# Two-layer network on one core: expert weights fetched one expert per slot in 4 KB rows, scatters in one batch

## The chip, the cores and the metric

The program runs on one core of one Trainium2 chip. The metric is the device time of one execution in microseconds (us). The core has a matrix engine (TensorE: PE for its matmuls, PEld for the loads of their stationary operand), a vector engine (DVE), an activation engine (ACT), GpSimd (POOL) and a queue engine (SP) that here only issues transfers. Sixteen DMA engines move data between the off-chip memory and the on-chip buffer of 128 partitions.

## What is computed

A token block of 256 rows and 1024 features goes through two layers, and then through a second block (forget-gate attention, a convolutional feed-forward and a gated addition). Each of the two layers has a mixer, a layer norm, a mixture of 16 experts, and a layer norm again. The experts are what the change touches:

```python
probs_g = softmax(xf @ w_group + b_group)              # 4 groups, the best one is taken
p_top, g_idx = top_k(probs_g, 1)
in_group = logits_e[group g_idx]                       # 4 experts of that group
w_top, e_local = top_k(softmax(in_group), 2)           # two of them
gates = p_top * w_top / sum(w_top)                     # zero for the other 14 experts
h = silu(x @ w_gate[e]) * (x @ w_up[e])                # 1024 -> 256, for each expert e
y = sum over e of (h * gates[e]) @ w_down[e]           # 256 -> 1024
```

All numbers are 32-bit floats. A layer has 16 x 3 x 1 MB of expert weights, and every expert's weights are read.

## The kernel before

`forward` (line 1230) runs a layer as mixer, output projection, `moe_slots` (line 728) and layer norm. In `moe_slots` the 256 tokens are two halves `tt` of 128. Each expert has room for `CAP` = 32 tokens of each half. A matrix `Pm[tt]` of zeros and ones (token by expert place) is made from the routing; `gather` (line 750) multiplies the normed tokens, split into a high part `xh` and a low part `xl`, by it: for a block `k` of 128 features, the stationary operand is `xh[:, tt, ks]`, a block of 128 neighbouring features, and the result, features by 512 expert places, is written to `XG[tt][k]` with the layer norm's scale and offset, which are columns of the constant `cw` (`mix_col`).

The 16 experts are taken in four groups `q` of four. `gate_up(q, ks, tt)` multiplies, for each block `k` and each expert `i` of the group, the 32 gathered tokens by 128 rows of gate and up weights. The four experts' results lie in the four 32-partition strips of one bank of the accumulator, so four matmuls run beside one another. `hidden` applies the gate's silu and the token's weight, `turned` transposes, `expert_down(q, hf, tt)` multiplies by half `hf` (512 columns) of the down weights and splits the result into a high part `yh` and a low part `yl`, and `scatter` adds them to the token's rows with two matmuls (lines 926 and 927).

Weights come in slots of 1 MB (8 KB in each partition). One layer uses 48 of them, in this order for each group: eight for gate and up, four for down. They are taken from three sets of buffers, in the order that the string `ORDER` (line 25) writes out: 7 of a ring, 4 more of `moe_slots`, and 2 that a pair of activation tiles leaves free; 2 more come free when the gathers are done with `xh` and `xl`. A slot is filled again only when its reader is done, and SP issues the transfers one after the other, each waiting for its own slot. So 13 to 15 slots are ahead of PE.

- `gate_up4` (line 676) fills a slot with one feature block `k` of four experts: two transfers of 512 KB, in which each row that is moved at one time is 256 numbers, 1 KB.
- A down slot (line 960) holds 128 rows of 512 columns of four experts: rows of 2 KB.
- A gate and up slot comes free after `gate_up` of its `k` for the second half; the slots of a group come free one by one.

PE's order is written out by hand (`seq` keeps it). After the first gathers: `gate_up(0, 0..3, 0)`, the other gathers, `gate_up(0, 0..3, 1)`, the weights of the scatter (lines 884 and 885), and then for each group: the rest of `gate_up`, **two blocks of the next group's `gate_up` for the first half** (line 964), the two transposes, the two `late` scatters of the group before, three `expert_down`, two scatters, the fourth `expert_down`. The last group ends with its own four scatters in two lots. At `q == 1`, `then` loads the next layer norm's two parameter rows, 512 KB each, over POOL's queue.

The scale row `gnb` of the first mixer (`hgrn`) is loaded in `consts`, at the start, on ACT's queue.

Of the kernel before, what the change touches and what calls it, by code (L numbers as in the profile page):

```python
# [8 lines left out]
F32 = mybir.dt.float32  # L9
# [37 lines left out]
class Net:  # L47
# [35 lines left out]
    def consts(self):  # L83
# [10 lines left out]
        self.gnb = t([P, 768], F32, "gnb")  # L94
        nc.scalar.dma_start(self.gnb, I["a_gnorm"][0].partition_broadcast(P))
# [352 lines left out]
    def hgrn(self, xT, wk):  # L448
        nc, I, V = self.nc, self.I, self.nc.vector
        W = I["a_w_in"][0]  # L450
        mm = nc.tensor.matmul
        Ss, Sm = [], []
# [11 lines left out]
        for j in range(3):  # L464
# [75 lines left out]
            nc.gpsimd.tensor_tensor(gs, gs, self.gnb[:, None, j * 256:j * 256 + 256].to_broadcast([P, 2, 256]),  # L540
# [187 lines left out]
    def moe_slots(self, xs, stats, lnw, layer, proj, then):  # L728
# [3 lines left out]
        with self.work() as wk:  # L732
# [16 lines left out]

            def gather(tt, k, dve):  # L750

                if k % 2 == 0:
                    XGT[tt].append(self.spl_tile(("hi", "lo")[tt], F32))
                ks = slice(k * P, (k + 1) * P)
# [5 lines left out]
                gc, bc = (self.mix_col(layer, n, k) for n in range(2))  # L760
# [5 lines left out]
            def lead():  # L766
# [49 lines left out]
                A, B = slice(0, 256), slice(256, 1024)  # L816
# [45 lines left out]
            def gate_up(q, ks, tt):  # L862

                for k in ks:
                    if (q, k) not in gu:
                        gu[q, k] = self.gate_up4(slot(), layer, q, k)
# [9 lines left out]
            for k in range(4):  # L876
                gu[0, k] = self.gate_up4(slot(), layer, 0, k)
# [34 lines left out]
            def expert_down(q, hf, tt):  # L912

                yb = self.bank()
                for f in range(2):
                    for i in range(4):
                        seq(mm(yb[CAP * i:CAP * i + CAP, :], hT[tt][:, f, CAP * i:CAP * i + CAP],  # L917
                               wd[q][2 * hf + f][:, i], start=f == 0, stop=f == 1))
                yh = wk.tile([P, 512], F32R, tag="yh", name=self.nm("yh"), bufs=2)
                yl = wk.tile([P, 512], F32R, tag="yl", name=self.nm("yl"), bufs=2)  # L920
# [453 lines left out]
```

## Time and profile before

| | |
|---|---|
| time, median of 3 runs | 965.22 us (964.32 to 966.99) |
| the profiled execution | 964.35 us, its span 962.8 us |
| PE busy | 880.5 us, 91% of the span |
| PE's weight loads | 652.9 us, 68% |
| DVE, ACT, POOL busy | 54%, 40%, 4% |
| moved by DMA | 207.09 MB, mean 215 GB/s |
| clock granted to PE | 0.962 of full speed on average |

The span is what the profiler saw of one execution; the time reported for that execution is 1.55 us longer. PE's share of busy time is an average over stages with quite different limits. The stages are told apart by the 40 slices of the profile's second part: the mixers, projections and the feed-forward move 54 to 250 GB/s, and in the two expert stages (about 203 to 318 us and 473 to 588 us) the DMA line stands at 350 to 370 GB/s.

### The profile page before, as it was taken

To read this page: it belongs to the slowest core of one execution; us is meant where nothing else is said; L and a number is where in the kernel's file an instruction comes from. 1 tells how busy PE (TensorE), PEld (TensorE's weight loads), DVE (VectorE), ACT (ScalarE), POOL (GpSimd) and SP (SyncE) were. 2 spreads that over 40 slices of the span, in tenths; PEclk is the share of its full clock that TensorE was granted. 3 is DMA by queue.
4 is the path that set the end of the run, shared out by engine and by line. 5 is a ranking of instruction groups with operands and counts; after the bars stand their busy time and mean duration, and the time that the engine had idled before them with its cause. 6 is when DMAs were issued, how large, how long until landed. Compare 5 with 4: busy or idle time off the path is not lost.

```text
span 962.8 us, 16096 instructions
## 1 busy us (share of the span) xinstructions
PE 880.5 (91%) x6733; PEld 652.9 (68%) x6733; DVE 517.3 (54%) x859; ACT 388.8 (40%) x628; POOL 36.8 (4%) x85
## 2 busy tenths in 40 slices
PE   5999989999869799989997697999998999999996
PEld 5899978742223497767532134888777999999975
DVE  5577784662101855655521027564468656656685
ACT  4443744351001355543611013564455545545531
POOL 2010110000000100000000000000000000000000
PEclk9999999999879899999897898999999999999998
DMA  9944335959999963319599999633245755556201
GB/s 320 350 137 149 116 119 178 321 189 368 352 362 372 339 203 109 102 54 302 176 364 352 366 365 351 221 132 100 88 133 181 254 176 176 185 170 214 88 1 69
DMA packets 163391, 207.09 MB, mean 215 GB/s; under 512 B 10231, under 2 KB 132719, under 8 KB 163311
## 3 DMA queue, kind: packets, MB, share of 16 engines
q1 hardware_dynamic: 162416, 203.43, 63.7%
q0 software_dynamic: 576, 2.10, 0.6%
q8 instruction: 55, 0.90, 0.4%
q10 hardware_dynamic: 318, 0.45, 0.2%
q14 instruction: 26, 0.21, 0.1%
HBM read 204.91 MB, written 1.05 MB: 214 GB/s over the span
## 4 chain that ended last, share of the span: by engine, by line
PE 81%; DVE 6%; DMA 6%; ACT 3%; issue 2%; POOL 1%; SPq 0%; ACTq 0%; POOLq 0%; DVEq 0%
PE pb L869 11%; PE pb L199 9%; PE pb L201 9%; PE pb L200 9%; PE pb L205 8%; PE pb L207 8%; PE pb L206 8%; PE pb L917 5%; DMA w<-in_w_up_dram 4%; PE pb L1004 2%; DVE lo L189 1%; DMA fx_wf<-in_attn_w_in_dram 1%; PE pb L271 1%; ACT hi L187 1%; PE pb L756 1%
## 5 line engine op out<-in xcount | busy, mean ns | idle before, releaser
L189 DVE TENSOR_TENSOR lo<-w,hi 128x1024 fp32r<-128x1024 f32 x151 | 184.2, 1223 | 102.0 <-ACT hi L187 101.0
L187 ACT ACTIVATE hi<-w 128x1024 fp32r<-128x1024 f32 x151 | 158.8, 1057 | 131.5 <-PE pb L201 63.2
L199 PE MATMUL pb<-th,hi 128*128 128x256 f32 x728 | 210.1, 289 | 0.7 <-ACT hi L187 0.6
L200 PE MATMUL pb<-th,lo 128*128 128x256 f32 x728 | 209.4, 288 | 0.7 <-DVE lo L189 0.7
L201 PE MATMUL pb<-tl,hi 128*128 128x256 f32 x728 | 208.8, 287 | 0.0
L199 PEld LDWEIGHTS pb<-th,hi 128*128 128x128 f32 x728 | 141.5, 194 | 4.7 <-issue 2.9
L200 PEld LDWEIGHTS pb<-th,lo 128*128 128x128 f32 x728 | 141.5, 194 | 2.5 <-issue 1.1
L201 PEld LDWEIGHTS pb<-tl,hi 128*128 128x128 f32 x728 | 141.6, 194 | 2.0 <-issue 2.0
L205 PE MATMUL pb<-hi,th 128*128 128x256 f32 (+1 forms) x308 | 107.8, 350 | 2.4 <-ACT th L261 1.4
L207 PE MATMUL pb<-hi,tl 128*128 128x256 f32 (+1 forms) x308 | 107.0, 347 | 0.3 <-DVE tl L262 0.3
L206 PE MATMUL pb<-lo,th 128*128 128x256 f32 (+1 forms) x308 | 106.8, 347 | 0.0
L869 PE MATMUL pb<-w,hi 128*32 128x512 f32 x512 | 67.2, 653 | 28.0 <-DMA w<-in_w_up_dram 28.0
L205 PEld LDWEIGHTS pb<-hi,th 128*128 128x128 f32 x308 | 59.8, 194 | 9.3 <-ACT th L261 2.3
L207 PEld LDWEIGHTS pb<-hi,tl 128*128 128x128 f32 x308 | 59.2, 192 | 9.3 <-DVE tl L262 2.0
L261 ACT ACTIVATE yh<-pb 128x512 fp32r<-128x512 f32 x32 | 19.1, 598 | 112.6 <-PE pb L917 100.5
L206 PEld LDWEIGHTS pb<-lo,th 128*128 128x128 f32 x308 | 59.5, 193 | 6.8 <-issue 0.7
L869 PEld LDWEIGHTS pb<-w,hi 128*32 128x32 f32 x512 | 16.0, 115 | 69.8 <-issue 67.3
L869 PE MATMUL pb<-w,lo 128*32 128x512 f32 x512 | 59.0, 592 | 0.0
L917 PE MATMUL pb<-w,hT 128*32 128x512 f32 x512 | 58.3, 596 | 0.6 <-DVE hT L909 0.6
L189 DVE TENSOR_TENSOR wdl<-w,wdh 128x1024 fp32r<-128x1024 f32 x25 | 30.5, 1224 | 39.1 <-ACT wdh L187 39.1
L262 DVE TENSOR_TENSOR yl<-pb,yh 128x512 fp32r<-128x512 f32 x32 | 22.1, 690 | 53.5 <-ACT yh L261 53.5
L187 ACT ACTIVATE wdh<-w 128x1024 fp32r<-128x1024 f32 x25 | 26.4, 1059 | 48.4 <-PE pb L207 44.4
(334 smaller groups left out, 1190.5 us busy)
## 6 DMA issues: line engine op xcount, KB each, us to landing
w<-in_w_gate_dram SPq DMA_DIRECT2D x64, 512.0 KB, 9.0
w<-in_w_up_dram SPq DMA_DIRECT2D x64, 512.0 KB, 8.8
w<-in_w_down_dram SPq DMA_DIRECT2D x32, 1024.0 KB, 11.3
w<-in_ffn_w_up_dram SPq DMA_DIRECT2D x22, 1024.0 KB, 5.1
w<-in_a_w_in_dram SPq DMA_DIRECT2D x13, 1024.0 KB, 10.0
w<-in_attn_w_in_dram SPq DMA_DIRECT2D x12, 1024.0 KB, 8.5
w<-in_ffn_w_down_dram SPq DMA_DIRECT2D x11, 1024.0 KB, 4.9
w<-in_w_o_dram SPq DMA_DIRECT2D x8, 1024.0 KB, 5.0
```

The lines of the kernel that those rows point to most:

```text
L187: a = nc.scalar.activation(h, src, AF.Copy)
L189: b = nc.vector.tensor_sub(l, src, h)
L199: mm(out, ah, bh, start=first, stop=False)
L200: mm(out, al, bh, start=False, stop=False)
L201: mm(out, ah, bl, start=False, stop=last)
L205: mm(out, xh, wh, start=first, stop=False)
L206: mm(out, xh, wl, start=False, stop=False)
L207: mm(out, xl, wh, start=False, stop=last)
L262: i = self.nc.vector.tensor_sub(l, ps, h)
L869: seq(mm(gb[q][tt][CAP * i:CAP * i + CAP, :], XG[tt][k][:, c:c + CAP], gu[q, k][:, i], start=k == 0, stop=k == KT - 1))
L917: seq(mm(yb[CAP * i:CAP * i + CAP, :], hT[tt][:, f, CAP * i:CAP * i + CAP], wd[q][2 * hf + f][:, i], start=f == 0, stop=f == 1))
L1004: nc.tensor.matmul(o(h), v[:, 0, vc(h)], ATs[h][:, 0:256], start=True, stop=False)
```

## The change

- A gate and up slot holds one expert (`gate_up_rows`): half `g` of its 1024 features, for gate and up. Partition `p` gets the four neighbouring rows `512 g + 4 p` to `512 g + 4 p + 3`, which are 4 KB in one piece in memory. Four slots (`fetch(q, g)`) are one half of a group. A transfer is 512 KB as before, in 128 rows of 4 KB.
- So block `k` of the features is no longer 128 neighbours, but every fourth one of 512: `gather` takes its stationary operand with a step of 4 numbers (`rows4`), and the scale and offset columns come from a new constant `mixp`, loaded at the start in the same order by four transfers on ACT's queue, 16 bytes at a time.
- A down slot holds one expert's whole down weight: 256 rows of 4 KB, one transfer of 1 MB.
- PE's order: the two blocks of the next group ahead of `turned` are gone; all four scatters of a group are late, and run as one batch in the next group after its first `turned`. For that `yh` and `yl` have three buffers instead of two, and the fourth pair uses the buffers of `Pm`.
- `gnb` is loaded in `hgrn`'s own buffers.
- The low and high parts in `lead` are made in two pieces of 512 columns instead of 256 and 768.

```diff
@@ consts
-        self.gnb = t([P, 768], F32, "gnb")
-        nc.scalar.dma_start(self.gnb, I["a_gnorm"][0].partition_broadcast(P))
+        self.mixp = t([P, 2, 2, 8], F32, "mixp")
+        for i, n in enumerate(("ln_mix_g", "ln_mix_b")):
+            for layer in range(2):
+                nc.scalar.dma_start(self.mixp[:, layer, i].rearrange("p (g r) -> p g r", g=2),
+                                    I[n][layer].rearrange("(g p r) -> p g r", g=2, r=4))
@@ hgrn
+        gnb = wk.tile([P, 768], F32, tag="gnb", name=self.nm("gnb"))
+        nc.scalar.dma_start(gnb, I["a_gnorm"][0].partition_broadcast(P))
@@
-    def gate_up4(self, slot, layer, q, k):
-        v = slot.rearrange("p (e c) -> p e c", e=4)
+    def gate_up_rows(self, slot, layer, e, g):
+        v = slot.rearrange("p (w r c) -> p w r c", w=2, r=4)
         for i, w in enumerate(("w_gate", "w_up")):
-            self.nc.sync.dma_start(v[:, :, i * 256:(i + 1) * 256],
-                                   self.I[w][layer, 4 * q:4 * q + 4, k * P:(k + 1) * P].rearrange("e p c -> p e c"))
+            self.nc.sync.dma_start(v[:, i], self.I[w][layer, e, 512 * g:512 * g + 512].rearrange("(p r) c -> p r c", r=4))
         return v
@@ moe_slots
+            def rows4(x, tt, k):
+                return x[:, tt, 512 * (k // 4):512 * (k // 4) + 512].rearrange("t (p r) -> t r p", r=4)[:, k % 4]
...
-                seq(mm(gb, xh[:, tt, ks], Pm[tt], start=True, stop=False))
-                seq(mm(gb, xl[:, tt, ks], Pm[tt], start=False, stop=True))
+                seq(mm(gb, rows4(xh, tt, k), Pm[tt], start=True, stop=False))
+                seq(mm(gb, rows4(xl, tt, k), Pm[tt], start=False, stop=True))
...
-                A, B = slice(0, 256), slice(256, 1024)
+                A, B = slice(0, 512), slice(512, 1024)
...
+            def fetch(q, g):
+                gu[q, g] = [self.gate_up_rows(slot(), layer, 4 * q + i, g) for i in range(4)]
+
+            def gate_up(q, g, tt):
+                if (q, g) not in gu:
+                    fetch(q, g)
+                for k in range(4 * g, 4 * g + 4):
                     for i in range(4):
                         c = (4 * q + i) * CAP
-                        seq(mm(gb[q][tt][CAP * i:CAP * i + CAP, :], XG[tt][k][:, c:c + CAP], gu[q, k][:, i],
-                               start=k == 0, stop=k == KT - 1))
+                        seq(mm(gb[q][tt][CAP * i:CAP * i + CAP, :].rearrange("p (w c) -> p w c", w=2),
+                               XG[tt][k][:, c:c + CAP], gu[q, g][i][:, :, k % 4], start=k == 0, stop=k == KT - 1))
...
             for q in range(4):
+                sg = []
                 if q:
-                    gate_up(q, range(2), 1)
-                    gate_up(q, range(2, 4), 0)
-                    gate_up(q, range(2, 4), 1)
-                gate_up(q, hi4, 0)
-                sg = [hidden(q, 0)]
-                gate_up(q, hi4, 1)
-                sg.append(hidden(q, 1))
+                    gb[q] = [self.bank("j"), self.bank("j")]
+                    for tt in range(2):
+                        gate_up(q, 0, tt)
+                for tt in range(2):
+                    gate_up(q, 1, tt)
+                    sg.append(hidden(q, tt))
                 if q == 1:
                     then()
                 wd[q] = []
-                for n in range(4):
-                    wd[q].append(slot().rearrange("p (e c) -> p e c", e=4))
-                    nc.sync.dma_start(wd[q][n], I["w_down"][layer, 4 * q:4 * q + 4, n % 2 * P:(n % 2 + 1) * P,
-                                                            n // 2 * 512:(n // 2 + 1) * 512].rearrange("e p c -> p e c"))
-                if q < 3:
-                    gb[q + 1] = [self.bank("j"), self.bank("j")]
-                    gate_up(q + 1, range(2), 0)
-                hT = [turned(sg[tt]) for tt in range(2)]
+                for i in range(4):
+                    wd[q].append(slot().rearrange("p (f c) -> p f c", f=2))
+                    nc.sync.dma_start(wd[q][i], I["w_down"][layer, 4 * q + i].rearrange("(f p) c -> p f c", p=P))
+                hT = [turned(sg[0])]
                 for y in late:
                     scatter(q - 1, *y)
-                if q < 3:
-                    y = [expert_down(q, 0, 0), expert_down(q, 0, 1), expert_down(q, 1, 0)]
-                    for n in range(2):
-                        scatter(q, *y[n])
-                    late = [y[2], expert_down(q, 1, 1)]
...
+                if q:
+                    hT.append(turned(sg[1]))
+                late = [expert_down(q, hf, 0) for hf in range(2)]
+                if not q:
+                    hT.append(turned(sg[1]))
+                late.append(expert_down(q, 0, 1))
+                if q == 3:
+                    for y in late[:2]:
+                        scatter(q, *y)
+                late.append(expert_down(q, 1, 1))
+            for y in late[2:]:
+                scatter(3, *y)
```

## Rows read from the trace of the kernel before

**Rows 1.** The page's part 4, the chain that ended last: shares by engine, by line.
```profile
PE 81%; DVE 6%; DMA 6%; ACT 3%; issue 2%; POOL 1%; SPq 0%; ACTq 0%; POOLq 0%; DVEq 0%
PE pb L869 11%; PE pb L199 9%; PE pb L201 9%; PE pb L200 9%; PE pb L205 8%; PE pb L207 8%; PE pb L206 8%; PE pb L917 5%; DMA w<-in_w_up_dram 4%; PE pb L1004 2%; DVE lo L189 1%; DMA fx_wf<-in_attn_w_in_dram 1%; PE pb L271 1%; ACT hi L187 1%; PE pb L756 1%
```

**Rows 2.** Line 869 (gate and up matmuls): PE's idle time before them (releaser: us, times).
```profile
  DMA w<-in_w_up_dram: 28.0, 8
```

**Rows 3.** The chain, layer 0's expert stage: start us, us, engine, tile, line, count.
```profile
202.11 3.57 PE pb L869 x32
...
236.93 9.34 DMA w<-in_w_up_dram
...
246.40 1.93 PE pb L869 x8
...
259.41 12.06 PE pb L869 x112
...
271.55 9.65 DMA w<-in_w_up_dram
...
308.77 5.29 PE pb L917 x48
...
317.60 1.06 ACT hi L187
```

**Rows 4.** The chain, layer 1's expert stage.
```profile
471.41 3.57 PE pb L869 x32
...
541.54 9.34 DMA w<-in_w_up_dram
...
587.26 1.06 ACT hi L187
```

**Rows 5.** SP's queue in time: transfers issued (start us, us of issue, line, tile, count).
```profile
201.90 0.37 SPq L960 DMA_DIRECT2D w<-in_w_down_dram  x1
203.17 0.53 SPq L680 DMA_DIRECT2D w<-in_w_gate_dram  x1
...
472.46 0.37 SPq L680 DMA_DIRECT2D w<-in_w_gate_dram  x1
```

**Rows 6.** Windows: us, engines' busy (x), granted clock, DMA share, GB/s. 1 KB, then 2 KB rows.
```profile
293.00:294.00 1.00, 1.00 (x16) 0.39 (x12) 0.00 (x0) 0.00 (x0) 0.00 (x0) 1.00 1.11 350
...
265.00:266.00 1.00, 1.00 (x12) 0.26 (x8) 0.00 (x0) 0.00 (x0) 0.00 (x0) 1.00 1.06 389
...
269.00:270.00 1.00, 1.00 (x16) 0.30 (x12) 0.00 (x0) 0.00 (x0) 0.00 (x0) 1.00 1.04 383
```

**Rows 7.** Windows of lone 1 MB transfers: 4 KB rows (feed-forward down), then 1 KB rows (up).
```profile
842.07:842.57 0.50, 0.50 (x4) 0.38 (x4) 0.50 (x1) 0.05 (x1) 0.00 (x0) 1.00 0.97 401
842.57:843.07 0.50, 0.50 (x4) 0.41 (x3) 0.50 (x2) 0.00 (x0) 0.00 (x0) 1.00 1.05 434
843.07:843.57 0.50, 0.50 (x4) 0.34 (x3) 0.39 (x1) 0.00 (x0) 0.00 (x0) 1.00 1.01 418
...
850.07:850.57 0.50, 0.50 (x6) 0.50 (x6) 0.50 (x2) 0.46 (x2) 0.00 (x0) 1.00 1.09 387
```

**Rows 8.** The DMA view: the layer norm parameters that `then` loads, over POOL's queue.
```profile
lng<-in_ln_ffn_g_dram POOLq DMA_DIRECT2D x2, 512.0 KB, 7.1
```

**Rows 9.** A window within the first stall: PE's granted clock is the third number from the right.
```profile
245.00:246.00 1.00, 0.00 (x0) 0.00 (x0) 0.00 (x0) 0.00 (x0) 0.00 (x0) 0.50 1.10 348
```

**Rows 10.** Gather's loads (ns min/median/max); a chain row of gather; a window where loads fill PEld.
```profile
L756 PEld LDWEIGHTS pb<-Pm,th x32: 186/188/333, 189.1 to 470.5; 128*128 128x128 f32 x32
...
198.15 0.23 PE pb L757
...
340.00:350.00 10.00, 10.00 (x83) 9.88 (x82) 5.34 (x5) 5.28 (x8) 0.00 (x0) 1.00 0.79 263
```

**Rows 11.** A transfer of 1024 rows of 64 bytes: its issue on SP, and a window it fell in.
```profile
576.19 2.50 SPq L1092 DMA_DIRECT2D fx_wf<-in_attn_w_in_dram  x1
...
585.00:586.00 1.00, 1.00 (x12) 0.26 (x8) 1.00 (x3) 0.00 (x0) 0.00 (x0) 1.00 1.11 315
```

**Rows 12.** The timeline at the start: ACT's first work, and the DVE row the chain passes through.
```profile
3.19 1.28 ACT L261 ACT_TABLE_LOAD   x1 [3.19 <-issue]
...
9.43 0.68 DVE L262 TENSOR_TENSOR tl<-pb,th 128x512 fp32r<-128x512 f32 x1
```

More of the change, by code (lines that the diff above doesn't have):

```diff
@@ L539, in hgrn @@
                     V.tensor_mul(gs[:, tt], gb[tt], gs[:, tt])
-            nc.gpsimd.tensor_tensor(gs, gs, self.gnb[:, None, j * 256:j * 256 + 256].to_broadcast([P, 2, 256]),
+            nc.gpsimd.tensor_tensor(gs, gs, gnb[:, None, j * 256:j * 256 + 256].to_broadcast([P, 2, 256]),
                                     op=ALU.mult)
@@ L753, in gather @@
                     XGT[tt].append(self.spl_tile(("hi", "lo")[tt], F32))
-                ks = slice(k * P, (k + 1) * P)
                 gb = self.bank("a")
-                seq(mm(gb, xh[:, tt, ks], Pm[tt], start=True, stop=False))
-                seq(mm(gb, xl[:, tt, ks], Pm[tt], start=False, stop=True))
+                seq(mm(gb, rows4(xh, tt, k), Pm[tt], start=True, stop=False))
+                seq(mm(gb, rows4(xl, tt, k), Pm[tt], start=False, stop=True))
                 o = XGT[tt][k // 2][:, k % 2 * 512:k % 2 * 512 + 512]
                 XG[tt].append(o)
-                gc, bc = (self.mix_col(layer, n, k) for n in range(2))
+                gc, bc = (self.mixp[:, layer, n, k:k + 1] for n in range(2))
                 if dve:
@@ L860, in lead @@
                 yield
[L862 to L866, printed above, removed]
+            def fetch(q, g):
[4 more added lines that the diff above has]
+                for k in range(4 * g, 4 * g + 4):
                     for i in range(4):
                         c = (4 * q + i) * CAP
-                        seq(mm(gb[q][tt][CAP * i:CAP * i + CAP, :], XG[tt][k][:, c:c + CAP], gu[q, k][:, i],
-                               start=k == 0, stop=k == KT - 1))
+                        seq(mm(gb[q][tt][CAP * i:CAP * i + CAP, :].rearrange("p (w c) -> p w c", w=2),
+                               XG[tt][k][:, c:c + CAP], gu[q, g][i][:, :, k % 4], start=k == 0, stop=k == KT - 1))
             hook = lead()
@@ L875, in moe_slots @@
             gb[0] = [self.bank("j"), self.bank("j")]
-            for k in range(4):
-                gu[0, k] = self.gate_up4(slot(), layer, 0, k)
+            fetch(0, 0)
             proj(hook)
@@ L917, in expert_down @@
                         seq(mm(yb[CAP * i:CAP * i + CAP, :], hT[tt][:, f, CAP * i:CAP * i + CAP],
-                               wd[q][2 * hf + f][:, i], start=f == 0, stop=f == 1))
-                yh = wk.tile([P, 512], F32R, tag="yh", name=self.nm("yh"), bufs=2)
-                yl = wk.tile([P, 512], F32R, tag="yl", name=self.nm("yl"), bufs=2)
+                               wd[q][i][:, f, hf * 512:hf * 512 + 512], start=f == 0, stop=f == 1))
+                if hf and tt:
+                    yh, yl = (wk.tile([P, 512], F32R, tag=f"Pm{n}", name=self.nm("y")) for n in range(2))
+                else:
+                    yh, yl = (wk.tile([P, 512], F32R, tag=n, name=self.nm("y"), bufs=3) for n in ("yh", "yl"))
                 with self.boost(3):
@@ L927, in scatter @@
                 seq(mm(acc[tt][hf], PT[tt][:, q], yl, start=False, stop=q == 3))
-            lo4, hi4 = range(4), range(4, 8)
-            gate_up(0, lo4, 0)
-            for k in lo4:
+            gate_up(0, 0, 0)
+            for k in range(4):
                 gather(1, k, k % 2 == 0)
-            for k in hi4:
+            for k in range(4, 8):
                 for tt in range(2):
@@ L937, in moe_slots @@
                 gates.append(next(rt[tt]))
-            gate_up(0, lo4, 1)
+            gate_up(0, 0, 1)
             for tt in range(2):
```

7 lines of the change are left out of this document (removed).

## The prediction

> **What bounds the kernel now.** I read the chain that ended last first. PE holds 81% of it, but one entry there is a transfer, the up weights with 4% of the span [rows 1]. Then I asked line 869 what PE waited for: 28.0 us of idle time in 8 waits for those weights [rows 2]. The chain in order of time shows where: in each layer twice, at 236.93 and 271.55 us in layer 0, and in the same places of layer 1 [rows 3, 4]. Both stand in the two blocks of `gate_up` that are pulled ahead of `turned` (line 964): PE waits for weights of the next group while the scatters and down products of the present group are ready to run.
>
> Next the windows over this stage. With gate and up weights in the queue (1 KB rows) the DMA share is 1.1 and the rate 350 GB/s; where the queue reaches down weights (2 KB rows) it is 383 GB/s [rows 6]. This holds from about 209 to 318 us without a pause: the expert stage is bound by the transfers, and it moves faster with the longer rows. [...]
>
> The stage can be written as a sum. From SP's first issue into a freed ring slot, at 203.17 us [rows 5], up to the slot whose landing ends the second stall, 25 slots go through: 17 of gate and up at 1.0486 MB / 348 GB/s = 3.01 us (348 is the rate of nearly every window of this kind), 8 of down at 1.0486 MB / 387 GB/s = 2.71 us; and the layer norm's 1 MB (two 512 KB parameter loads, [rows 8]), 2.7 us. That is 75.6 us, so 278.8 us; the landing is at 271.55 + 9.65 = 281.2 us [rows 3]. The 2.4 us left over are latency. In layer 1 the same sum from the issue at 472.5 us [rows 5] gives 548.1 against 550.9 us [rows 4]. The model holds to half a microsecond; I use it for the change.
>
> **The change, part by part.**
>
> *Longer rows (main term).* The bytes stay the same; what a slot costs depends on the rate at 4 KB. From below: the 2 KB rate, 383 to 389 GB/s, 387 taken [rows 6]. From above: a lone 1 MB transfer with 4 KB rows, 401 to 434 GB/s in its full half-microsecond windows, the mean of three 418 [rows 7]. Between: a packet of 1 KB takes 1024 x 16 / 348 = 47.1 ns on each of 16 engines, one of 2 KB 84.7 ns; the line through both gives 160 ns for 4 KB, 410 GB/s. A lone transfer with 1 KB rows reaches 387 [rows 7] where a queue of them holds 348, so queues run below bursts; I take 405, and 387 to 418 as its ends. A slot then costs 2.59 us (2.51 to 2.71).
>
> [...]
>
> *Later, coarser release (against it).* Now a ring slot comes free after each block of features; then four come free together at the end of `gate_up(0, 0, 1)`: 202.11 + 3.57 = 205.7 us [rows 3], so SP starts at 205.8, not 203.17. Left are slots 13 to 47 without the down slot that needs only `xh` free (issued at 201.90 now [rows 5], and again): 34, plus the parameters: 35 x s. The last four landed are down weights, and each `expert_down` needs all four experts, so all the down products of the last group follow the last landing. Now that tail lies at 308.77 to 317.60 us, 8.8 us [rows 3], with the same order of work. End of layer 0's stage: 205.8 + 35 s + 2.4 + 8.8 = 217.0 + 35 s. At 2.59 us it is 307.6, against 317.6 now: 10.0 us less. Layer 1: 475.1 + 90.6 + 2.6 + 8.8 = 577.1 against 587.3 [rows 4]: 10.2 less.
>
> Does the queue stay full? PE's own work from 202.1 to 317.6 is 115.5 us less 14 us of idleness (half of [rows 2]) less about 4.6 us lost at half clock, some 97 us, 24 us for 12 slots: 2.0 us a slot against 2.59 for its transfer. PE frees slots faster than they are refilled, and 13 to 15 slots are 34 to 39 us of transfer, more than the 7 to 10 us for which four wait for their common release.
>
> *Stall ahead of `turned` removed.* No gain on top: the stall is the transfers' time and is in the sum. It moves. PE runs `turned`, scatters and down products first, then waits at `gate_up(q + 1, 0, 0)` or near the last group, for some 4 us. If half clock is granted afterwards, as now [rows 9], the end slips: gate and up of the last half group, transposes, scatters and down products are 19 us of PE work behind its landing, as long as the last four transfers and the tail together. Eight matmuls at half clock took 1.93 us instead of 12.06 x 8/112 = 0.86 [rows 3]; between 0 and 2.4 us a layer, I take 1.
>
> *One batch of scatters.* Eight matmuls in one row instead of two lots of four save a change of operand form of about 0.3 us, three times a layer; PE is not the bound, so 0 taken, up to 2 us in all.
>
> *Strided stationary operand in `gather`.* 32 loads a layer step over 16 bytes; no load here does so. Loads that fill PEld follow each other at 0.12 us (82 in 9.88 us); a gather matmul takes 0.23 us and hides one [rows 10]. At twice the cost (0.24) a load adds 0.01 us; at four times (0.48) 0.25 us for 24 loads at full clock, 6 us a layer, all of it on the path, since SP waits for what follows. I take 0.3 us a layer (nearest to 0.12 doubled); the ends are 0 and 6.
>
> [...]
>
> *Start.* `mixp` is four transfers of 256 rows of 16 bytes. The nearest row is a transfer of 1024 short rows: 2.50 us of issue, and in three windows of 1 us around its landing the rate falls from 385 to about 315 GB/s (the row shown is the middle one in rate), 3 x 70/385 = 0.6 us of DMA time [rows 11]. On ACT's queue the issues (4 x 0.6 us, less `gnb`'s 0.5) push the table load from 3.19 to about 5 us; DVE's constants hold the chain until 9.43 us [rows 12], so it is hidden; without that cover 2 us. `gnb` moves to `hgrn`, behind whose 0.5 us issue only ACT stands, which is 40% busy. I take 0.3, ends 0 and 2. The 512 and 512 column pieces add 0.3 us ahead of the first gather, under PE's routing sums: 0.
>
> Sum: -10.0 - 10.2 + 2 x 1 + 2 x 0.3 + 0.3 = -17.3 us. From the profiled execution, 964.35 us, that is 947.0; the median of the runs is 0.9 higher, so 948 us.
>
> **The rivals.**
> 1. *The rate stays at that of 2 KB rows.* s = 2.71: the stage ends at 311.9, 5.7 us earlier; twice, with the same 2.9 us of costs: -8.5, about 956. For it: a ceiling of the memory could lie there. Against: lone 4 KB rows run above 400 [rows 7].
> 2. *Slower: coarse release without a better rate.* If long rows gain nothing in a full queue of gate and up weights (s = 3.01, 348 GB/s), the stage ends at 322.4, 4.8 us later in each layer: with the costs +12.5, about 978. It decides where 217.0 + 35 s passes 317.6: s = 2.87, 365 GB/s. Against: two row lengths side by side in one queue at 350 and 383 [rows 6]. [...]
> 3. *The step of 16 bytes costs four times as much.* +11.4 us on the forecast: 959; with rival 1, 967.
> 4. *SP blocks.* It issues in order; if a transfer whose four slots are late is placed ahead of others that could go, the queue drains: a slot's time, 2.6 us, for each of two batches in a layer, +10: 958.
> 5. *PE becomes the bound.* No stall, no half clock: 14 + 4.6 us a layer at most, 927; with 418 GB/s (-2.8 us a layer) and no slip, 940.
>
> **How the numbers follow.** Forecast (405 GB/s, small costs; 942 to 953) 0.50; rival 1 0.19; rivals 3 and 4 together 0.16, of which a third, where they meet rival 1, lands within 0.3% (about 3 us, what a measurement here can tell from no change) or just beyond; rival 2 0.07; rival 5 0.08. Faster 0.87, same 0.05, slower 0.08. The range from 938 to 960 leaves out rival 2, the worst of 3 and 4, and the best of 5.
>
> **What would show it.** Windows of the expert stage at 395 to 415 GB/s, with a DMA share below 1.05 (right), at 387 (rival 1) or 350 (rival 2). First issue after the gathers near 205.8 us; idle DMA windows after it would be rival 4. The chain's ACT row after the stage, now at 317.60, about 9 us earlier from the stage's start. Gather matmuls at 0.23 us apart, or 0.3 to 0.5 (rival 3). Waits of line 869 for weights below 15 us in all. I am wrong if 4 KB rows in a queue don't beat 2 KB rows, or if PE, not SP's queue, is late in the last group.

## The result and the profile after

The changed kernel takes 948.5 us (median of four executions, 947.4 to 948.7) against 965.9 us for the kernel before in the same session: a ratio of 0.982, with a 95% interval from 0.980 to 0.984. The forecast was 948.0. Its profiled execution took 948.71 us with a span of 946.9, so 15.9 us of span are gone. Lines have moved by 4 to 11: `gate_up`'s matmuls are now line 880 (869 before), `expert_down`'s 927 (917), the gather's 764 and 765 (756 and 757), the rounded copies `hi` (fp32r) of dense weights 191 (187), the evacuations `th` of transposes 265 (261).

The page's part 4 for the changed kernel, the chain that ended last, by engine and then by line (to be set beside [rows 1]):

```profile
PE 67%; DMA 17%; DVE 8%; ACT 5%; issue 2%; POOL 1%; SPq 0%; ACTq 0%; DVEq 0%; POOLq 0%
DMA w<-in_w_up_dram 11%; PE pb L205 9%; PE pb L203 9%; PE pb L204 8%; PE pb L209 7%; PE pb L211 7%; PE pb L210 7%; PE pb L880 5%; DMA w<-in_w_down_dram 3%; DVE lo L193 2%; PE pb L927 2%; PE pb L1011 2%; ACT hi L191 1%; PE pb L275 1%; DMA w<-in_a_w_in_dram 1%
```

The expert weights stand on the chain itself now, 11% and 3% of the span, where [rows 1] had 4%. PE's idle time ahead of line 880 in the changed kernel (releaser: us, times), against 28.0 us in [rows 2]:

```profile
  DMA w<-in_w_up_dram: 8.6, 8
```

More of the chain, and less waiting, is no contradiction: PE waits in short pieces, just behind the queue. The chain in order of time in the changed kernel (start us, us, what), layer 0's stage, and after the dots layer 1's, beside [rows 3, 4]:

```profile
208.47 3.57 PE pb L880 x32
215.51 8.82 PE pb L880 x64
225.56 10.31 DMA w<-in_w_up_dram
...
284.82 10.22 DMA w<-in_w_up_dram
...
295.17 7.03 PE pb L880 x58
...
304.64 6.02 PE pb L927 x48
...
314.28 1.06 ACT hi L191
...
466.18 3.57 PE pb L880 x32
...
473.23 7.12 PE pb L880 x64
...
541.54 10.22 DMA w<-in_w_up_dram
...
571.02 1.06 ACT hi L191
```

I measure a stage from the second `gate_up` of group 0 (the x32 row) to the first ACT copy behind it. Layer 0: 115.49 us before, 105.81 now. Layer 1: 115.85 before, 104.84 now. That is 20.7 us less in both. But the first stage begins at 208.47 instead of 202.11, 6.4 us later; between the stages 1.9 us are gained, and 0.3 lost after the second: 6.4 - 9.7 - 1.9 - 11.0 + 0.3 = -15.9, the whole difference of the spans.

Windows of the changed kernel (us, engines' busy, then granted clock, DMA share, GB/s), against [rows 6]: the stretch from the first gate issue to the landing at 295.04, two windows inside it, the one with the layer norm's parameters and its lowest part, one with these parameters in layer 1, and one at the only place in the stages where half clock is still granted ([rows 9] had it in the stalls):

```profile
212.05:295.04 82.99, 77.42 (x634) 27.52 (x634) 19.33 (x35) 12.34 (x23) 1.31 (x2) 0.98 1.02 405
...
250.00:260.00 10.00, 10.00 (x100) 2.92 (x92) 2.77 (x4) 2.39 (x4) 0.00 (x0) 1.00 1.03 408
...
270.00:280.00 10.00, 10.00 (x74) 4.62 (x70) 2.62 (x5) 1.58 (x4) 0.00 (x0) 1.00 1.02 408
...
220.00:230.00 10.00, 8.92 (x80) 2.73 (x76) 3.62 (x7) 1.96 (x4) 1.18 (x2) 1.00 1.03 389
...
227.00:228.00 1.00, 1.00 (x16) 0.34 (x11) 0.24 (x1) 0.60 (x1) 0.00 (x0) 1.00 1.13 303
...
480.00:490.00 10.00, 8.92 (x80) 2.85 (x80) 3.22 (x6) 2.70 (x5) 0.00 (x0) 1.00 1.02 409
...
216.00:218.00 2.00, 2.00 (x16) 0.52 (x12) 1.97 (x3) 1.30 (x2) 0.00 (x0) 0.50 1.02 408
```

The queue moves 407 to 411 GB/s in every window of 10 us from 230 to 300 us, where [rows 6] had 350 and 383 to 389. Layer 0 has one weak place ahead of that: SP issues no weights from 217.2 to 224.2 us, and from 227 to 230 us the rate is 303 to 352. Layer 1 has the same parameters in its queue, but no half clock (1.00 throughout) and no such dip (385 GB/s in its lowest window of 1 us up to 545 us). SP's issues in the changed kernel (start us, us, line, tile, count): the first after the gathers in each layer, beside [rows 5], and the last four down slots of layer 0:

```profile
208.27 1.53 SPq L971 DMA_DIRECT2D w<-in_w_down_dram  x2
212.05 0.34 SPq L686 DMA_DIRECT2D w<-in_w_gate_dram  x1
...
286.14 4.21 SPq L971 DMA_DIRECT2D w<-in_w_down_dram  x4
...
469.76 0.34 SPq L686 DMA_DIRECT2D w<-in_w_gate_dram  x1
```

The gather's loads in the changed kernel (ns min/median/max), beside [rows 10]: the load with a step of 16 bytes takes 311 ns where the contiguous one took 188.

```profile
L764 PEld LDWEIGHTS pb<-Pm,th x32: 307/311/331, 195.1 to 465.3; 128*128 128x128 f32 x32
```

And the start, ACT's timeline in the changed kernel, against [rows 12], and behind the dots PE's second lot of the block's transposes:

```profile
3.73 2.49 ACTq L98 DMA_DIRECT2D mixp<-in_ln_mix_b_dram  x2
6.32 0.42 ACTq L457 DMA_DIRECT2D gnb<-in_a_gnorm_dram  x1
6.77 1.28 ACT L191 ACT_TABLE_LOAD   x1 [6.77 <-DMA mixp<-in_ln_mix_b_dram]
10.73 2.00 ACT L191 ACTIVATE hi<-w 128x1024 fp32r<-128x1024 f32 x2 [2.67 <-DMA w<-in_a_w_in_dram]
15.61 2.00 ACT L191 ACTIVATE hi<-w 128x1024 fp32r<-128x1024 f32 x2 [2.88 <-DMA w<-in_a_w_in_dram]
17.51 1.06 ACT L265 ACTIVATE th<-pb 128x512 fp32r<-128x512 f32 x2
...
18.87 1.97 PE L275 MATMUL pb<-ident,x 128*128 128x128 f32 x8 [12.12 <-DVE tl L266]
```

The same instructions in the kernel before, the first and the last of four evacuations, and the copies behind them:

```profile
6.10 0.60 ACT L261 ACTIVATE th<-pb 128x512 fp32r<-128x512 f32 x1 [1.62 <-PE pb L271]
...
12.17 0.60 ACT L261 ACTIVATE th<-pb 128x512 fp32r<-128x512 f32 x1 [0.26 <-PE pb L271]
12.67 3.89 ACT L187 ACTIVATE hi<-w 128x1024 fp32r<-128x1024 f32 x4
```

The order on ACT is turned round. Before, `th` came first (6.1 to 12.8 us) and the copies `hi` followed; now the copies stand ahead, the second pair waits for its weights until 15.6, and the `th` of the block's transposes, which PE needs first, are behind them from 17.5 on. PE waits 12.1 us for what follows from `th`. `hgrn`'s first sigmoid starts at 31.7 us instead of 22.7.

### The profile page after: what moved, and what is told of

It is laid out like the page before. It is cut to its first block, busy times and chain, and to the rows that moved or that the text cites. A ratio compares the mean times of both kernels' runs of the same rounds, so it can differ in the third digit from the quotient of the medians.

```text
span 946.9 us, 16120 instructions
## 1 busy us (share of the span) xinstructions
PE 876.8 (93%) x6733; PEld 659.6 (70%) x6733; DVE 517.6 (55%) x859; ACT 388.8 (41%) x628; POOL 36.8 (4%) x85
## 3 DMA queue, kind: packets, MB, share of 16 engines
HBM read 204.93 MB, written 1.05 MB: 218 GB/s over the span
## 4 chain that ended last, share of the span: by engine, by line
PE 67%; DMA 17%; DVE 8%; ACT 5%; issue 2%; POOL 1%; SPq 0%; ACTq 0%; DVEq 0%; POOLq 0%
DMA w<-in_w_up_dram 11%; PE pb L205 9%; PE pb L203 9%; PE pb L204 8%; PE pb L209 7%; PE pb L211 7%; PE pb L210 7%; PE pb L880 5%; DMA w<-in_w_down_dram 3%; DVE lo L193 2%; PE pb L927 2%; PE pb L1011 2%; ACT hi L191 1%; PE pb L275 1%; DMA w<-in_a_w_in_dram 1%
## 5 line engine op out<-in xcount | busy, mean ns | idle before, releaser
L205 PE MATMUL pb<-tl,hi 128*128 128x256 f32 x728 | 208.5, 287 | 0.0
L880 PE MATMUL pb<-w,hi 128*32 128x512 f32 x512 | 70.1, 608 | 9.1 <-DMA w<-in_w_up_dram 8.6
L880 PE MATMUL pb<-w,lo 128*32 128x512 f32 x512 | 62.7, 592 | 0.0
L927 PE MATMUL pb<-w,hT 128*32 128x512 f32 x512 | 60.4, 595 | 2.2 <-ACT sg L908 1.1
L880 PEld LDWEIGHTS pb<-w,hi 128*32 128x32 f32 x512 | 18.8, 112 | 52.9 <-issue 49.3
L908 ACT ACTIVATE sg<-pb 128x256 f32<-128x256 f32 x16 | 6.1, 383 | 104.8 <-PE pb L880 104.8
L909 DVE SCALAR_TENSOR_TENSOR sg<-pb,r_gs,sg 128x256 f32<-128x256 f32 x16 | 7.7, 479 | 73.4 <-ACT sg L908 73.4
## 6 DMA issues: line engine op xcount, KB each, us to landing
w<-in_w_gate_dram SPq DMA_DIRECT2D x64, 512.0 KB, 10.2
w<-in_w_up_dram SPq DMA_DIRECT2D x64, 512.0 KB, 10.2
```

The costliest lines, as they stand in the source:

```text
L205: mm(out, ah, bl, start=False, stop=last)
L880: seq(mm(gb[q][tt][CAP * i:CAP * i + CAP, :].rearrange("p (w c) -> p w c", w=2), XG[tt][k][:, c:c + CAP], gu[q, g][i][:, :, k % 4], start= ...
```

## The experiments

Two questions: why did the first stage begin 6.4 us late, and which of the change's parts shortened the stages? The first five kernels are for the start. One candidate is the four transfers of `mixp` in rows of 16 bytes. The other is the place of `gnb`'s load. The build keeps the first copy `hi` behind the instruction that was written just before it on ACT's queue (`self.pin = 1` in `forward`, used in `split`). Before, that was the last `th`; with `gnb` loaded at the top of `hgrn`, it is `gnb`'s transfer, and nothing holds `hi` behind `th` any more.

**s1_gnb_later**: `gnb`'s two lines moved within `hgrn`, on the changed kernel.

```diff
-        gnb = wk.tile([P, 768], F32, tag="gnb", name=self.nm("gnb"))
-        nc.scalar.dma_start(gnb, I["a_gnorm"][0].partition_broadcast(P))
...
             if j == 0:
+                gnb = wk.tile([P, 768], F32, tag="gnb", name=self.nm("gnb"))
+                nc.scalar.dma_start(gnb, I["a_gnorm"][0].partition_broadcast(P))
                 kv = self.mem_kv(0)
```

> The changed kernel with one load moved: the gated norm's weights (gnb) are fetched in the first pair of heads, just ahead of the memory values, instead of at the top of the recurrent mixer. All else as in the changed kernel, the four short-row loads of the norm's parameters at the start included. What is asked: layer 0's expert stage began at 208.5 us in the changed kernel and at 202.1 in the kernel before, 6.4 us late. Theory A, the order on ACT: in the changed kernel ACT makes the bf16 copies of the first projection weights (15.6 us on) ahead of the four transposes' evacuations (17.5 us on), in the kernel before the evacuations came first (6 to 12 us); with this load moved the evacuations come first again, the stage begins 5 to 6 us sooner, and the time is 942 to 944 us. Theory B, the short rows of the norm's parameters take the DMA engines' time at the start: nothing of that is changed here, so the stage still begins near 208 us and the time is 947 to 949.

Measured: 941.6 us (938.9 to 942.9), ratio 0.977 (0.975 to 0.980). ACT's timeline of this kernel, and after the dots its chain, the rows that begin and end layer 0's stage:

```profile
8.42 1.09 ACT L265 ACTIVATE th<-pb 128x512 fp32r<-128x512 f32 x2
11.30 0.60 ACT L265 ACTIVATE th<-pb 128x512 fp32r<-128x512 f32 x1 [1.80 <-PE pb L275]
12.16 0.60 ACT L265 ACTIVATE th<-pb 128x512 fp32r<-128x512 f32 x1 [0.26 <-PE pb L275]
12.65 1.99 ACT L191 ACTIVATE hi<-w 128x1024 fp32r<-128x1024 f32 x2
...
200.25 3.57 PE pb L880 x32
...
305.23 1.06 ACT hi L191
```

`th` is ahead of `hi` again, the stage begins at 200.3, and the time is 5.8 us below that of s3, the kernel with the late start that was measured beside it (6.9 below the changed kernel's, which was measured beside slower executions of the kernel before: 965.9 us there, 963.6 here).

**s2_before_mixp**: `mixp`'s four transfers added to the kernel before, which doesn't use them.

```diff
+        self.mixp = t([P, 2, 2, 8], F32, "mixp")
+        for i, n in enumerate(("ln_mix_g", "ln_mix_b")):
+            for layer in range(2):
+                nc.scalar.dma_start(self.mixp[:, layer, i].rearrange("p (g r) -> p g r", g=2),
+                                    I[n][layer].rearrange("(g p r) -> p g r", g=2, r=4))
```

> The kernel before with one thing added: the four short-row loads of the norm's parameters (16-byte rows) on ACT's queue at the start. The kernel does not use what they bring. Theory A, the order on ACT: that order is as in the kernel before, so the loads cost their issues and some engine time beside other transfers only, 0 to 2 us: layer 0's stage begins at 202 to 204 us and the time is 965 to 967. Theory B, the short rows are the whole of the late start: 6 us, a stage begin near 208, 971 us.

Measured: 963.3 us beside 963.6 for the kernel before, ratio 0.999 (0.998 to 1.001). The stage begins at 199.9. The short rows cost nothing here.

**s3_mixp_late**: on the changed kernel, the four transfers away from the start; `gnb` as in the change.

```diff
-                nc.scalar.dma_start(self.mixp[:, layer, i].rearrange("p (g r) -> p g r", g=2),
-                                    I[n][layer].rearrange("(g p r) -> p g r", g=2, r=4))
...
+            nc.sync.dma_start(self.mixp[:, layer, i].rearrange("p (g r) -> p g r", g=2),
+                              I[n][layer].rearrange("(g p r) -> p g r", g=2, r=4))
```

> The changed kernel with the four short-row loads of the norm's parameters taken from the start and put, two for each layer, beside the router's loads on SP's queue. The gated norm's weights stay where the change put them. Theory A, the order on ACT: the bf16 copies still go ahead of the four evacuations, the stage still begins 4 to 6 us late (206 to 208 us), 946 to 949. Theory B, the short rows at the start: without them the stage begins at 202 to 203 us, and the time is 942 to 943.

Measured: 947.4 us, ratio 0.983 (0.981 to 0.985); the copies `hi` at 11.2 to 16.2 us, the first `th` at 16.1, the stage from 206.8. Most of the late start stays without the short rows. Not quite all: `th` comes 1.4 us sooner than in the changed kernel and the stage 1.7, so behind the turned order the short rows may cost up to that much; the ratios, 0.983 and 0.982, don't show it.

**s4_both**: the edits of s1 and s3 together.

> The changed kernel with both moves: the gated norm's weights fetched in the first pair of heads, and the four short-row loads put beside the router's loads on SP's queue, two for each layer. Theory A (order on ACT) and theory B (short rows) both give a stage that begins at 202 to 203 us here, and 941 to 943 us; what this tells is whether the two together are all of the 6.4 us. If the stage still begins at 206 us or later, a third cause is at work, and the time is 946 to 949.

Measured: 941.6 us (940.5 to 942.8), ratio 0.977 (0.975 to 0.979), the stage from 201.9. With s1's time in the same session the same to 0.1 us, `mixp` at the start costs nothing once the order is mended, and that order is, as far as these times tell, what made the start late.

**s5_before_gnb**: the other way round, `gnb`'s load moved to the top of `hgrn` in the kernel before.

```diff
-        self.gnb = t([P, 768], F32, "gnb")
-        nc.scalar.dma_start(self.gnb, I["a_gnorm"][0].partition_broadcast(P))
...
+        gnb = wk.tile([P, 768], F32, tag="gnb", name=self.nm("gnb"))
+        nc.scalar.dma_start(gnb, I["a_gnorm"][0].partition_broadcast(P))
...
```

> The kernel before with one part of the change alone: the gated norm's weights are fetched at the top of the recurrent mixer instead of among the constants at the start. Nothing of the expert stage is touched. Theory A, this move turns round the order on ACT: the bf16 copies of the first projection weights stand ahead of the four evacuations, the first stage begins 4 to 6 us later than in the kernel before (206 to 208 us against 202.1), and the time is 967 to 971. Theory B, the late start needs more of the change than this move: the order on ACT and the time stay, 962 to 966.

Measured: 967.1 us, ratio 1.004 (1.002 to 1.006). ACT's timeline of this kernel:

```profile
11.07 2.00 ACT L185 ACTIVATE hi<-w 128x1024 fp32r<-128x1024 f32 x2 [6.65 <-DMA w<-in_a_w_in_dram]
14.08 2.00 ACT L185 ACTIVATE hi<-w 128x1024 fp32r<-128x1024 f32 x2 [1.01 <-DMA w<-in_a_w_in_dram]
15.99 1.06 ACT L259 ACTIVATE th<-pb 128x512 fp32r<-128x512 f32 x2
```

This move alone turns the order round, with no `mixp` in the kernel, and costs 3.8 us. The place was off: the first sigmoid is 6.0 us late (28.7), but the stage begins only 1.8 us late (203.95), and the rest is spread over the stages and what lies between them. How much of a late start survives until 200 us differs from kernel to kernel. Over all the traces, the kernels with `th` first begin the stage at 199.8 to 202.1 us, those with `hi` first and the rest of the change at 206.7 to 208.5, and this one stands between. Sign and order are settled; why the same turn costs less here is not.

The others undo the parts that concern the stages. All lengths are in the table behind them.

**r1_rows1k**: s4 with rows of 1 KB. One expert per slot and the order of the slots stay.

```diff
-            self.nc.sync.dma_start(v[:, i], self.I[w][layer, e, 512 * g:512 * g + 512].rearrange("(p r) c -> p r c", r=4))
+            self.nc.sync.dma_start(v[:, i], self.I[w][layer, e, 512 * g:512 * g + 512].rearrange("(r p) c -> p r c", r=4))
...
-                seq(mm(gb, rows4(xh, tt, k), Pm[tt], start=True, stop=False))
+                seq(mm(gb, xh[:, tt, k * P:(k + 1) * P], Pm[tt], start=True, stop=False))
...
```

> The changed kernel with the start mended (gated norm's weights and norm parameters moved as in s4_both) and one part undone: gate and up weights arrive in 1 KB rows with the features in their natural order (contiguous gather, parameters by feature block), still one expert per slot, in the same order of slots; the down weights keep 4 KB rows. s4_both with 4 KB rows has stages of 106.4 and 104.7 us and 941.6 us. Theory A, the row length sets the rate: 23 gate and up slots lie between the stage's first issue and its last landing, each 3.01 us at the 348 GB/s of [rows 6] in place of 2.56 at 410, so each stage is about 10 us longer (115 to 117), the 1 KB windows show 345 to 355 GB/s, and the time is 960 to 963. Theory B, the gain came from the coarser slots (half as many issues and releases) or their order: stages of 105 to 107 and 941 to 944 us, with the transfers no slower than now.

Measured: 963.6 us, ratio 1.000 (0.999 to 1.001). A window of its stage:

```profile
250.00:260.00 10.00, 9.02 (x80) 2.84 (x72) 1.37 (x2) 0.60 (x1) 0.00 (x0) 1.00 1.09 348
```

The rate is the old 348 and the time is the old time. The whole change is in this kernel but for the row length of gate and up and the gather's step that goes with it; the start is mended besides. Without the long rows nothing is left of the gain, though the down weights still come in 4 KB rows. The stages are 9.7 and 11.9 us longer than s4's, where 23 slots x (3.01 - 2.56) us make 10.4.

**r2_rows2k**: s4 with rows of 2 KB; `rows4` and `mixp` take the same order (not shown).

```diff
-            self.nc.sync.dma_start(v[:, i], self.I[w][layer, e, 512 * g:512 * g + 512].rearrange("(p r) c -> p r c", r=4))
+            self.nc.sync.dma_start(v[:, i].rearrange("p (h r) c -> p h (r c)", h=2),
+                                   self.I[w][layer, e, 512 * g:512 * g + 512].rearrange("(h p r) c -> p h (r c)", h=2, r=2))
```

> As r1_rows1k, but with gate and up in 2 KB rows (two neighbouring features per row, the gather stepped by two, the norm parameters in the order that goes with it). Theory A, the row length sets the rate: 23 slots of 2.71 us at the 387 GB/s that 2 KB rows had in the kernel before, against 2.56 at 410, so each stage is 3 to 4 us longer than in s4_both (108 to 110), the windows show 383 to 390 GB/s, and the time is 947 to 950. Theory B, all that matters is to leave 1 KB rows: stages of 105 to 107, 941 to 943. The gather's loads, stepped by 2 elements, should last between the 188 ns of step 1 and the 311 of step 4, and change nothing of the time.

Measured: 950.2 us, ratio 0.988 (0.985 to 0.990); 387 GB/s in its windows of gate and up. The gather's loads with a step of 8 bytes:

```profile
L764 PEld LDWEIGHTS pb<-Pm,th x32: 193/197/333, 186.7 to 461.7; 128*128 128x128 f32 x32
```

**o1_hoist**: the changed kernel with the pull ahead of `turned` put back, here one `gate_up(q + 1, 0, 0)`.

```diff
-                    gb[q] = [self.bank("j"), self.bank("j")]
-                    for tt in range(2):
-                        gate_up(q, 0, tt)
+                    gate_up(q, 0, 1)
...
+                if q < 3:
+                    gb[q + 1] = [self.bank("j"), self.bank("j")]
+                    gate_up(q + 1, 0, 0)
                 hT = [turned(sg[0])]
```

> The changed kernel with one part undone: the first gate and up half of the next group is again pulled ahead of the turning of the hidden values, as in the kernel before. Theory A, PE runs behind the transfers in the stage, and its order inside a group decides nothing: stages of 104 to 107 us as in the changed kernel (105.8 and 104.8) and 947 to 950 us. Theory B, the order matters: with the pull, slots come free at other times and the half ahead waits for its weights; stages longer by 2 us or more each, 952 us or above. Theory C, the pull was worth something and the change lost it: stages 1 to 2 us shorter, 945 to 946.

Measured: 967.8 us (964.2 to 970.0), ratio 1.004 (1.002 to 1.007): 19.2 us above the changed kernel, 21 above o2, its near relative in the same session, and slower than the kernel before. Three views of this kernel: what SP waited for at the down slots' issue in layer 0 (us in total, times, longest), the issue of the last group's four, and a window:

```profile
SPq L969 <- PE pb L927: 33.7, 3, 13.6
...
289.19 16.15 SPq L969 DMA_DIRECT2D w<-in_w_down_dram  x4
...
300.00:305.00 5.00, 5.00 (x52) 1.49 (x48) 1.84 (x4) 1.79 (x3) 0.00 (x0) 1.00 0.04 8
```

The same wait in the changed kernel:

```profile
SPq L971 <- PE pb L927: 2.9, 1, 2.9
```

Here PE stands ahead of all four slots of the next half group while the four down slots of the present group are held. SP's next down transfers need those very buffers, and queue behind PE's products (line 927): 16.15 us for the last four issues instead of the 4.21 of the changed kernel. The queue runs dry: 8 GB/s in the window, and 238 and 251 in the two from 235 to 245 us.

**o3_rows1k_pull**: r1 with the same pull, to tell slots from rows.

> r1_rows1k (one expert per slot, 1 KB rows, mended start; stages of 116.2 and 116.6 us, 963.6 us) with the pull of o1_hoist. The pull cost nothing with the old slots and 1 KB rows (the kernel before against b1_before_nopull) and 19 us with the new slots and 4 KB rows (the changed kernel against o1_hoist); slots and rows differ between the two. Theory A, the slots: with one expert per slot PE stands before all four slots of the next half group while the four down slots are held, SP's next down transfers wait for PE, and the queue runs dry; with 1 KB rows four slots take 12 us in place of 10.4, so each of the three pauses is a little shorter than in o1_hoist: stages of 120 to 126 us and 972 to 984. Theory B, the rows: the pauses come only where the queue is faster than PE's freeing of slots, and at 350 GB/s there are none: stages of 115 to 118, 962 to 967.

Measured: 982.3 us, ratio 1.019 (1.017 to 1.022). The wait of the down slots' issue in this kernel:

```profile
SPq L968 <- PE pb L926: 26.7, 3, 9.8
```

The pull costs 19 us at 1 KB too (982.3 against 963.6), so the row length is not what makes it dear; what the two have in common is the slots.

**b1_before_nopull**: the pull taken out of the kernel before.

```diff
                 if q:
-                    gate_up(q, range(2), 1)
+                    gb[q] = [self.bank("j"), self.bank("j")]
+                    for tt in range(2):
+                        gate_up(q, range(2), tt)
...
-                if q < 3:
-                    gb[q + 1] = [self.bank("j"), self.bank("j")]
-                    gate_up(q + 1, range(2), 0)
```

> The kernel before with one part of the change alone: the first two feature blocks of the next group are no longer pulled ahead of the turning of the hidden values; rows of 1 KB and the old slots stay. o1_hoist showed that the changed kernel loses 19 us with a pull. Theory A, the pull costs only with the new slots, four of which come free together: here the queue has no pause with or without the pull, PE's two waits of 10 to 12 us in a layer move to other places, the stages stay at 114 to 117 us and the time at 962 to 967. Theory B, the order is a gain of its own, whatever the slots: stages shorter by 3 us or more, 958 or below. Theory C, the pull helped here: stages longer by 2 us or more, 969 or above.

Measured: 962.4 us, ratio 0.999 (0.998 to 1.001). With slots of one feature block the pull neither helps nor hurts. It was two blocks there, half the PE work of o1's, since a slot of one expert can't be had for less than four together; how much of the 19 us is due to that size was not tried.

**o2_scatter_split**: the changed kernel with the scatters two and two.

```diff
+                if q < 3:
+                    y = [expert_down(q, 0, 0)]
...
+                    for n in range(2):
+                        scatter(q, *y[n])
+                    late = [y[2], expert_down(q, 1, 1)]
+                    continue
...
```

> The changed kernel with the scatters split again: two of a group's four follow its own down products and two those of the next group, instead of all four in one batch a group later. Theory A, in the first three groups PE has time to spare behind the transfers, and where the scatters stand decides nothing: stages 105 to 107 us, 947 to 950 us. Theory B, the batch saves changes of shape between products: stages 1 to 2 us longer each, 950 to 953 us. Theory C, the split frees PE's banks sooner: 945 to 947.

Measured: 946.8 us, ratio 0.984 (0.981 to 0.987), not to be told from the change's 0.982. The batch is worth nothing that shows. The change of operand form that it was to save is in the trace of the kernel before: at 224.05 us the first scatter matmul starts 0.52 us after the last of `expert_down`, where the next four of these start after 0.41, and at 224.39 and 225.18 us two more starts come 0.33 us after the one ahead, where 0.23 is usual: about 0.3 us in all.

| kernel | gate/up rows | slot | pull | stage, layer 0 | layer 1 | time, us |
|---|---|---|---|---|---|---|
| before | 1 KB | feature block | yes | 115.5 | 115.9 | 963 to 966 |
| b1_before_nopull | 1 KB | feature block | no | 116.8 | 115.7 | 962.4 |
| o3_rows1k_pull | 1 KB | expert | yes | 126.0 | 125.8 | 982.3 |
| r1_rows1k | 1 KB | expert | no | 116.2 | 116.6 | 963.6 |
| r2_rows2k | 2 KB | expert | no | 109.0 | 108.1 | 950.2 |
| o1_hoist | 4 KB | expert | yes | 118.2 | 111.8 | 967.8 |
| the change | 4 KB | expert | no | 105.8 | 104.8 | 948.5 |
| s4_both | 4 KB | expert | no | 106.4 | 104.7 | 941.6 |
| s1_gnb_later | 4 KB | expert | no | 105.0 | 104.7 | 941.6 |

The kernels with the prefix r, and o3, have the mended start of s4. The change's own time is from a session in which the kernel before took 965.9 us; in the others it took 963.1 to 963.6. The best version is the change with s1's edit: 0.977 of the kernel before.

## Why the prediction was right, and where it was not

**Longer rows: right.** The forecast had 405 GB/s in a full queue, between 387 and 418; the full windows show 407 to 411, and the whole stretch from 212.05 to 295.04 us, with its dip, 405. Over the slots the model holds as well: from the first issue at 212.05 us to the landing that PE waits for at 284.82 + 10.22 = 295.04 us are 83.0 us, less 2.4 of latency, for 30 slots (29 issued in that time, and the second of the two down slots issued just ahead of it) and the layer norm's parameters: 31 times 2.60 us; 2.59 was predicted. r1 and r2 show that the row length makes it, with the two prices that the windows of before already had: 348 and 387 GB/s. Rivals 1 and 2 fall with this.

**Later, coarser release: right in the changed order, unpriced outside it.** SP's first gate issue came 3.58 us after the stage's begin (3.7 predicted), and but for the dip of layer 0 the queue stayed full. The prediction argued that PE frees slots fast enough, 2.0 us against 2.59, and left it there. o1 and o3 show how little room there is: half a `gate_up` moved ahead of the down products, 3.6 us of PE work and its wait, and the same queue runs dry: with 4 KB rows the stages are 12.4 and 6.9 us longer (o1 beside the change).

**Stall ahead of `turned` removed: the step that was read wrongly.** The prediction put it at nothing on top of the transfers. For the kernel before that is so (b1), and for the sum it did no harm, since the sum assumed a full queue. But a part that costs nothing to add can still be what carries the rest: with the pull kept, the change would have been slower than before (o1, 967.8): its two stages together took 230 us against 231 before, and the late start came on top. The sentence should have named the down slots as what the pull would have held.

**The tail: right.** The stage ends 19.2 us after the last landing for which line 880 waits (295.04 to 314.28), as the forecast's 19; and by the prediction's sum, counted from this stage's begin, the last down slot is due at 208.47 + 96.7 = 305.2. PE's chain reaches the down products at 304.64, and there a weight load waits until 305.32 for that slot (start us, us, what, idle time before it and what ended that):

```profile
305.32 0.25 PEld L927 LDWEIGHTS pb<-w,hT 128*32 128x32 f32 x8 [0.60 <-DMA w<-in_w_down_dram]
```

Both paths end together, within a microsecond, as the prediction had it.

**Half clock: taken too dear.** 1 us a layer was put down for a slip behind a late stall. In the kernel before, layer 0's windows of 1 us show a granted clock of 0.50 from 245 to 251 us and from 276 to 285, in and behind the two stalls. PE was busy for 10.2 us of these 15, so at half speed some 5 us were lost there (an estimate from these windows), where the prediction had 4.6. After, no window of the last groups shows 0.50; PE's waits for weights add to 8.6 us in 8 pieces. Half clock is left at one place in layer 0 (0.50 from 216 to 219 us, 0.84 in the window behind), where 64 matmuls take 8.82 us instead of 7.12 in layer 1, and the slots that they free are issued that much later; s1, without it, has a stage 0.8 us shorter. So the stages gained 20.7 where the forecast, with its costs, had 17.6.

**Between the stages: 1.9 us that can't be put down to the change.** Before, the window from 455 to 460 us had a granted clock of 0.60, and the next 0.72; after, both had 1.00. But over all the traces this stretch takes 151.6 to 155.3 us whatever the kernel: 154.3 in s1, which has the change, 151.6 in b1, which has none of its rows or slots. The kernel before had 153.8 in its trace and the change 151.9, so this part is luck as far as the runs tell.

**Strided gather: right, by its cover.** The loads take 311 ns instead of 188 at the median, but a gather matmul follows the last after 0.24 us instead of [rows 10]'s 0.23: some 0.1 us a layer for 24 loads at full clock, near the lower end of 0 to 6. The rest is covered: the loads too begin 0.24 us apart, beside the matmuls. Rival 3 falls. A load took 188 ns at a step of 4 bytes, 197 at 8 (r2) and 311 at 16.

**Start: the term that was mis-sized.** 0.3 us were taken, 2 at most; it was 6.4. The `mixp` transfers were costed and are free where `th` comes first, as s2, s1 and s4 show, with the cover that was named (the table load ends at 8.4 us in s1, and the third `th` still starts at 11.3 as before), though they push that load further than was reckoned, to 7.1 us and not 5. What failed is the clause on `gnb`: it asked only what stands behind `gnb`'s issue on ACT, half a microsecond, and not what was held in place by the instructions around it. That is the one cost that was not foreseen, and it has nothing to do with the experts. The two pieces of 512 columns in `lead`, put at nothing, had no run of their own.

So the forecast of 948.0 stands beside 948.5 partly by luck, because errors cancel: the stages gave 20.7 us where 17.6 were summed, the stretch between them 1.9 where nothing was, and the start took 6.4 where 0.3 was. The mechanism in the stages, which carries the gain, is not luck.

**SP blocks, PE as the bound.** Rival 4 did not come about in the change, though o1 is that rival with PE's order as its cause. Rival 5 did not either: PE still waits for transfers in both stages, in layer 0 the last time for its last down slot. Two of the rivals' times, 956 and 927, leave out the 0.9 us that the forecast adds for the median; nothing hangs on it.

## What to carry to other kernels

Where a stage is bound by a full transfer queue, the length of the contiguous rows is worth asking about before anything else: layer 0's stage, with the same bytes in the same slots, took 116, 109 and 106 us with rows of 1, 2 and 4 KB. With coarser slots, follow each release through the engine's order: whatever waits for the next slots must not stand ahead of the work that frees the ones the queue needs next. And a load that is moved "for free" can be the anchor of a pinned order: compare the order on each engine at the place it left, not only what is queued where it went.

## What the runs showed of the hardware

- A full queue on SP of 512 KB transfers ran at 348 GB/s with 1 KB rows (before, r1), 387 with 2 KB (r2), 407 to 411 with 4 KB (the change), with a DMA share of about 1.10, 1.05 and 1.03; 348 was the same in slots of a feature block and of an expert.
- SP's own issue of such a transfer took 1.37 us (gate) and 1.35 (up) at the median with 1 KB rows (line 680 before, 0.37 at the least), and 0.33 and 0.42 with 4 KB (line 686 after). In r1 and b1 these issues stand on the chain, one after another at 1.4 us. SP itself is not that slow: in the kernel before, the first issues of the stage, into a queue that had run nearly empty, took 0.53, 0.50 and 0.63 us from 203.17 us on, and the 16 engines show a share of 1.10 at 348 GB/s ([rows 9]). That speaks for a full queue that holds SP back; no run was made for it.
- A 128x128 load of a 32-bit stationary operand: 188 ns at the median with neighbouring elements (before, r1), 197 with a step of two (r2), 311 with a step of four (the change).
